# One level of Strassen's algorithm for both products of each MLP, in a two-layer trunk

## The chip, the cores and the metric

The kernel runs on one NeuronCore of one Trainium2 chip. The metric is the device time of one execution in microseconds, as the median of several runs. The core has five engines that work side by side, each through its own instructions in order: PE (matrix products and transposes), DVE (vector arithmetic), ACT (activation functions and copies), POOL (vector arithmetic and software-made DMAs) and SP (which issues DMAs). ACT and POOL issue DMAs too.

## The reference

A trunk of two layers over x (1024 tokens of 1024 numbers), with a token mixer (RWKV-7 beside Mamba-2 in layer 0, an mLSTM in layer 1), a cross-attention into 256 memory tokens, and an MLP of width 4096. The change concerns the MLP.

```python
def squared_relu_mlp(h, w_up, w_down):
    return jnp.square(jax.nn.relu(h @ w_up)) @ w_down

for i in range(DEPTH):
    ...
    x = x + rmsnorm(mix, norm_mix_post[i])
    ...
    x = x + rmsnorm(ca, norm_xa_post[i])
    ff = squared_relu_mlp(rmsnorm(x, norm_ff_pre[i]), ff_up[i], ff_down[i])
    x = x + rmsnorm(ff, norm_ff_post[i])
```

## The kernel before

**Products.** An fp32 product is made of three fp32r matmuls. `split` (L215) cuts a number into a high part, which ACT copies into fp32r (L217), and a low part, which DVE subtracts (L218). `mm3` (L207) multiplies high by high, high by low and low by high into one PSUM bank, through `mm` (L201); transposes go through `tr` (L205). Tiles of x are 128 tokens, so there are eight; a matmul here is 128x128 weights with 512 columns.

**Order.** A tile framework places the waits, and its scheduler, which simulates the program, fixes the order of each engine's instructions. The program hands it an order of its own as well: generators put on a list by `bg` are advanced by `tick` and `until`, by a model time `pt` that each matmul moves on. This is how norms of one stage run beside products of another.

**Cross-attention's end** (`xattn`). For each token tile the output product goes into a PSUM tile of 1024 columns (`psd`), `postnorm` (L337 to L363) squares it on ACT (L351), multiplies by the gain on DVE (L352), makes the reciprocal root on POOL (L354, L356), adds the residual on DVE (L362) and stores (L363). `tail_norm` then normalises for the MLP (`prenorm`, L334), and eight transposes with copies give the transposed x as high and low parts, `xth` and `xtl`.

**MLP** (`mlp`). The hidden width is cut into 16 chunks of 256. `up(c)` makes two times 128 hidden rows for all 1024 tokens, 48 matmuls each (`fm`), with Relu on ACT (L1439), a square on DVE (L1440) and a split into `u`. `down` multiplies a chunk's `u` by two rows of weights into a PSUM bank for each of 8 tiles and 2 column halves, and `add` copies (L1461) or adds (L1463) it on DVE into `acc`, which stays in SBUF. up(c+1) stands ahead of down(c). Weights of both products come by DMAs that ACT issues (`wstream`, L231), 512 KB each, and are split into `wb`. The first two up products begin with tokens 0 to 511 (`fm_two`) and take the rest when the last tiles of the attention are ready. The last two chunks are paired so that the tiles finish one after another; `finish(t)` is the post-norm and, in layer 0, the norm and transposes for layer 1. Each product has 1536 matmuls a layer, so both products of both layers have 6144.

## Time and profile before

| what | value |
|---|---|
| median of 3 runs | 3235.38 us (3228.02 to 3237.13) |
| the profiled execution's own time | 3245.01 us |
| its span, first to last instruction | 3243.2 us |
| mean granted TensorE clock | 0.982 |
| busy: PE, DVE, ACT, POOL | 3121.8, 1610.6, 1025.1, 342.6 us |
| DMA traffic | 361.54 MB, mean 111 GB/s |

The rows come from one execution recorded by the profiler. The span starts at the first instruction; the MLP of layer 0 runs from about 1147 to 1860 us of it, that of layer 1 from about 2520 us to the end. A row of the timeline gives start, length, engine, line, operation, output and inputs, shape and count, and in brackets how long the engine was idle just before and what ended the wait. The rows of a view by stretches give, after the stretch, the busy time of PE, PE's weight loads, DVE, ACT and POOL with their counts, the granted clock (1.00 is 2.4 GHz), the share of the 16 DMA engines in use and GB/s.

### The profile page before, as it was taken

What the parts mean: (1) busy time and instruction counts of PE and PEld (TensorE: products, weight loads), DVE (VectorE), ACT (ScalarE), POOL (GpSimd) and SP (SyncE); (2) the same over time, 40 slices, a digit from 0 to 9 for tenths busy, and PEclk for the clock granted to TensorE, in tenths of its full rate; (3) what the DMA queues carried; (4) which work ended last, traced back from release to release, by engine and by line L of the source; (5) the groups of instructions that cost most, each with busy time, mean ns of one, the idle gap of its engine ahead of it and who ended that gap; (6) DMA issues with size and microseconds to landing.
All of it is one profiled execution on the core that took longest, in us unless ns stands there. A gap on an engine that the chain in (4) does not pass through costs nothing. (4 is left out here: it accounts for less than half of the span.)

```text
span 3243.2 us, 40057 instructions
## 1 busy us (share of the span) xinstructions
PE 3121.8 (96%) x16420; PEld 2535.6 (78%) x16420; DVE 1610.6 (50%) x2247; ACT 1025.1 (32%) x1684; POOL 342.6 (11%) x444
## 2 busy tenths in 40 slices
PE   8999997889989999999999999899999999999999
PEld 8777676777768878888888788777788788888887
DVE  7255788566543444444444713146634444444445
ACT  6556533445333321111111413133433211111112
POOL 1111121122221100000000200012211000000001
PEclk9999998899989999999999999999999999999999
DMA  7734465588451221111111323455322211111112
GB/s 257 256 94 124 126 181 172 192 265 276 153 179 53 85 94 43 52 52 46 51 40 47 123 85 119 123 167 186 125 85 78 78 52 52 46 46 39 52 52 110
DMA packets 236295, 361.54 MB, mean 111 GB/s; under 512 B 54208, under 2 KB 157056, under 8 KB 236112
## 3 DMA queue, kind: packets, MB, share of 16 engines
q1 hardware_dynamic: 178832, 165.43, 16.8%
q10 hardware_dynamic: 45984, 152.59, 14.1%
q0 software_dynamic: 11296, 40.97, 3.2%
q8 instruction: 129, 2.11, 0.3%
q14 instruction: 54, 0.44, 0.0%
HBM read 262.73 MB, written 96.17 MB: 111 GB/s over the span
## 5 line engine op out<-in xcount | busy, mean ns | idle before, releaser
L201 PE MATMUL pd<-xth,wb 128*128 128x512 f32 x3168 | 1023.9, 398 | 15.9 <-DVE wb L218 13.6
L201 PE MATMUL pm<-wb,u 128*128 128x512 f32 x3072 | 738.1, 391 | 0.4 <-DVE acc L1463 0.4
L201 PEld LDWEIGHTS pd<-xth,wb 128*128 128x128 f32 x3168 | 596.6, 189 | 165.6 <-DVE wb L218 17.0
L201 PEld LDWEIGHTS pm<-wb,u 128*128 128x128 f32 x3072 | 576.5, 188 | 128.0 <-DVE acc L1463 1.3
L201 PE MATMUL pd<-xtl,wb 128*128 128x512 f32 x1600 | 635.4, 398 | 0.8 <-DVE xtl L218 0.8
L1463 DVE TENSOR_TENSOR acc<-pm,acc 128x512 f32<-128x512 f32 x448 | 305.5, 689 | 403.7 <-PE pm L201 403.7
L217 ACT ACTIVATE wb<-wr 128x1024 fp32r<-128x1024 f32 x244 | 252.8, 1051 | 701.8 <-PE pm L201 412.2
L218 DVE TENSOR_TENSOR wb<-wr,wb 128x1024 fp32r<-128x1024 f32 x244 | 295.4, 1224 | 227.9 <-ACT wb L217 227.4
L201 PEld LDWEIGHTS pd<-xtl,wb 128*128 128x128 f32 x1600 | 300.6, 188 | 73.3 <-issue 2.4
L201 PE MATMUL pd<-w,sh 128*128 128x512 f32 x1024 | 325.7, 400 | 8.6 <-DVE y L352 5.7
L201 PEld LDWEIGHTS pd<-w,sh 128*128 128x128 f32 x1024 | 193.6, 191 | 51.6 <-ACT w L217 5.9
L1440 DVE TENSOR_TENSOR ur<-ur 128x1024 f32<-128x1024 f32 x64 | 78.3, 1224 | 312.9 <-ACT ur L1439 312.9
L201 PE MATMUL pd<-w,sl 128*128 128x512 f32 x512 | 204.2, 399 | 0.0
L1439 ACT ACTIVATE ur<-pd 128x1024 f32<-128x1024 f32 x64 | 65.6, 1025 | 400.4 <-PE pd L201 400.4
L354 POOL TENSOR_SCALAR r<-ssh 128x1 f32<-128x1 f32 x48 | 25.4, 530 | 1553.8 <-ACT j L351 1553.0
L201 PE MATMUL pm<-wb,xth 128*128 128x512 f32 x512 | 163.1, 399 | 1.7 <-ACT wb L217 1.7
L201 PEld LDWEIGHTS pm<-wb,xth 128*128 128x128 f32 x512 | 96.6, 191 | 23.4 <-ACT wb L217 2.1
L201 PEld LDWEIGHTS pd<-w,sl 128*128 128x128 f32 x512 | 97.6, 191 | 21.8
L201 PE MATMUL pm<-wb,xtl 128*128 128x512 f32 x256 | 101.9, 398 | 0.0
L201 PE MATMUL ph<-w,mh 128*128 128x512 f32 x256 | 87.7, 419 | 3.9 <-ACT mh L217 3.0
L201 PE MATMUL pd<-w,yth 128*128 128x512 f32 x256 | 85.4, 412 | 2.9 <-DVE y L352 1.6
L218 DVE TENSOR_TENSOR u<-ur,u 128x1024 fp32r<-128x1024 f32 x64 | 78.2, 1221 | 1.1 <-ACT u L217 1.1
(344 smaller groups left out, 3628.8 us busy)
## 6 DMA issues: line engine op xcount, KB each, us to landing
wr<-in_ff_upT_dram ACTq DMA_DIRECT2D x64, 512.0 KB
wr<-in_ff_down_dram ACTq DMA_DIRECT2D x64, 512.0 KB
scr<-xo POOLq DMA_DIRECT2D x39, 512.0 KB, 3.0
scr<-mo POOLq DMA_DIRECT2D x32, 512.0 KB, 5.6
xo<-scr SPq DMA_DIRECT2D x32, 512.0 KB
wr<-in_ev_fm_dram ACTq DMA_DIRECT2D x26, 512.0 KB
wr<-in_xa_wkT_dram ACTq DMA_DIRECT2D x16, 512.0 KB
wr<-in_xa_wvT_dram ACTq DMA_DIRECT2D x16, 512.0 KB
```

Of the source, the lines that this page charges most:

```text
L201: self.nc.tensor.matmul(out, lhsT=lhsT, rhs=rhs, start=start, stop=stop)
L217: self.nc.scalar.activation(hi, src, AF.Copy)
L218: self.nc.vector.tensor_tensor(lo, src, hi.bitcast(F32), ALU.subtract)
L354: nc.gpsimd.tensor_scalar(r1[:], ss[:, 0:1], ss[:, 1:2], NORM_EPS, ALU.add, ALU.add)
L1439: nc.scalar.activation(r[:], ps[:], AF.Relu)
L1440: nc.vector.tensor_tensor(r[:], r[:], r[:], ALU.mult)
L1463: nc.vector.tensor_tensor(acc[:, t, sl], ps[:], acc[:, t, sl], ALU.add)
```

## The change

Both products of each MLP are made by one level of Strassen's algorithm in the form with seven products. Every matrix is cut into two by two blocks; seven block products replace eight, with sums and differences of blocks before and after. A product then has 1344 matmuls a layer.

*First product.* `half_norm` (L1443) replaces `tail_norm`: all tiles go to `xraw` as fp32, and tiles 0 to 3 are split as well, into `b1` (blocks B11, B21). `x_sums` (L1475) makes the other five right operands B22 and T1 to T4 tile by tile: four DVE subtractions (L1483) and five splits for each of four pairs of tiles. `prep` (L1498) loads the two weight rows of a pair of hidden chunks (512 KB each, issued on SP) and makes the left operands with four DVE sums and three and a half splits. `pair` (L1539) makes the seven block products, 12 matmuls each, for 256 hidden rows, adds them in PSUM and in `ub` (L1550 to L1574) and applies Relu and Square, and four POOL operations (L1576 to L1579) make the left operands of the second product. One DMA stores the seven pieces, 1792 KB, to the DRAM buffer `U` (L1580). `ub` has two buffers, used by pairs in turn. The products A11 x B11 and A12 x B21 of pairs 0 and 1 stand ahead, where fm_two stood.

*Second product.* It begins when all 16 pairs are done. There are 56 steps a layer, seven products by eight, each with 24 matmuls. `load` (L1619) brings one piece of U (`ru`) and one of weights (`rw`), 512 KB each (L1626, on SP), one step ahead in program order, and splits them into `wb` (four buffers) for two steps in five and into `sx` (three buffers) for the other three. `mul` makes six matmuls for each of four token tiles in a step. Products that share a result are summed in PSUM banks; at a product's end four banks are copied by ACT or added by DVE into `CA` and `CB` (L1686 to L1699). Tiles 0 to 3 finish during the last two products, tiles 4 to 7 at the end.

*Weight sums.* `down_sums` (L1423) makes the four sums and differences of blocks of ff_down, for both layers, as a background generator from the kernel's start: 64 times 512 KB in on SP, four POOL subtractions of 128x256, 512 KB out on POOL's queue, into the DRAM buffers `WS`. ff_down is laid out in blocks in DRAM (`ff_dn`). The scratch space for software-made DMAs is set to 4096.

The diff, cut to its core:

```diff
+        raw = qx.tile([P, NK, T], F32, name=self.n("xraw"), tag="xth")
+        b1 = qx.tile([P, 2, NK, 512], F32R, name=self.n("xb1"), tag="xtl")
+        xt = raw, (b1[:, 0], b1[:, 1])
...
-            self.bg(self.tail_norm(xo, g_ff, xt[0][:, :, ts], xt[1][:, :, ts], fin, 9.0))
+            self.bg(self.half_norm(t, xo, g_ff, xt, fin, 9.0))
...
+    def down_sums(self, l):
+        nc = self.nc
+        sub = ALU.subtract
+        for p in range(16):
+            for h in range(2):
+                w = self.cp.tile([P, 4, 256], F32, name=self.n("ws"), tag="ws")
+                cs = slice(256 * h, 256 * h + 256)
+                nc.sync.dma_start(w[:], self.A["ff_dn"][l, :, p // 2, :, p % 2, cs].rearrange("b p c -> p b c"))
+                yield 10.0
+                a1, a2, b1, b2 = [w[:, i, :] for i in range(4)]
+                op = lambda out, x, y: nc.gpsimd.tensor_tensor(out, x, y, sub)
+                op(a1, a2, a1)
+                op(a2, b2, a2)
+                op(b2, b2, a1)
+                op(b1, b1, b2)
+                nc.gpsimd.dma_start(self.WS[l][:, p // 2, :, p % 2, cs].rearrange("b p c -> p b c"), w[:])
+                yield 15.0
+        self.ws_done[l] = True
...
+            if t < 4:
+                self.split(hi[:, ks, ts], lo[:, ks, ts], v)
+            self.nc.scalar.copy(raw[:, ks, ts], v)
...
+        wb = self.pool(ca, "wb", 4, side)
...
+        def x_sums():
+            for t in range(4):
+                yield lambda: 0.0 if cond(t + 5) else None
+                yield 1.5
+                c = slice(P * t, P * t + P)
+                r11, r21 = [raw[:, 4 * i:4 * i + 4, c] for i in range(2)]
+                r12, r22 = [raw[:, 4 * i:4 * i + 4, 512 + P * t:640 + P * t] for i in range(2)]
+                sp = lambda k, src: self.split(X[k][0][:, :, c], X[k][1][:, :, c], src)
+                op = lambda out, x, y: nc.vector.tensor_tensor(out, x, y, sub)
+                sp("B22", r22)
+                op(r11, r12, r11)
+                op(r12, r22, r12)
+                op(r22, r22, r11)
+                sp("T2", r22)
+                sp("T1", r11)
+                op(r21, r21, r22)
+                sp("T3", r12)
+                sp("T4", r21)
...
+        def prep(p):
+            d = {}
+            fa = self.wr.tile([P, 1024], F32, name=self.n("wr"), tag="wr")
+            nc.sync.dma_start(fa[:], A["ff_upT"][l, 2 * p])
+            fb = self.ed.tile([P, 1024], F32, name=self.n("wf"), tag="gain")
+            nc.sync.dma_start(fb[:], A["ff_upT"][l, 2 * p + 1])
+            def first():
+                t1 = sp2()
+                self.split(t1[:, 0], t1[:, 1], fa[:])
+                d["A11"], d["A12"] = cut(t1)
+            def rest():
+                s = self.ed.tile([P, 1024], F32, name=self.n("ws"), tag="xn")
+                nc.vector.tensor_tensor(s[:, lo], fb[:, lo], fb[:, hi], add)
+                nc.vector.tensor_tensor(s[:, hi], s[:, lo], fa[:, lo], sub)
+                t2 = sp2()
+                self.split(t2[:, 0], t2[:, 1], s[:])
+                d["S1"], d["S2"] = cut(t2)
+                if "A11" not in d:
+                    first()
+                s4 = self.ed.tile([P, 1024], F32, name=self.n("ws"), tag="xo")
+                nc.vector.tensor_tensor(s4[:, lo], fa[:, lo], fb[:, lo], sub)
+                nc.vector.tensor_tensor(s4[:, hi], fa[:, hi], s[:, hi], sub)
+                t3 = sp2()
+                self.split(t3[:, 0], t3[:, 1], s4[:])
+                d["S3"], d["S4"] = cut(t3)
+                t4 = sp2()
+                self.split(t4[:, 0, lo], t4[:, 1, lo], fb[:, hi])
+                d["A22"] = t4[:, 0, lo], t4[:, 1, lo]
+            return d, first, rest
...
+        def prod(ps, w, x, start=True):
+            for k in range(4):
+                c = slice(P * k, P * k + P)
+                self.mm3(ps, (w[0][:, c], w[1][:, c]), (x[0][:, k, :], x[1][:, k, :]), start and k == 0, k == 3, not start)
...
+        def pair(p, d, early=None, ahead=None):
+            u = ub[:, p % 2]
+            sl = lambda i: u[:, i, :]
+            if early is None:
+                ab = self.psd()
+                a, b = ab[:, lo], ab[:, hi]
+            else:
+                (a, a2), b = early, self.psm()[:]
+            c = self.psm()[:]
+            prod(b, d["S2"], X["T2"])
+            nc.scalar.copy(sl(7), b)
+            prod(c, d["S1"], X["T1"])
+            if ahead is not None:
+                ahead()
+            if early is None:
+                prod(a, d["A11"], X["B11"])
+            nc.scalar.copy(sl(3), a)
+            nc.vector.tensor_tensor(sl(7), sl(7), sl(3), add)
+            prod(b, d["S3"], X["T3"], False)
+            nc.vector.tensor_tensor(sl(2), b, sl(3), add)
+            nc.vector.tensor_tensor(sl(2), c, sl(2), add)
+            if early is None:
+                prod(a, d["A12"], X["B21"], False)
+                nc.scalar.activation(sl(0), a, AF.Relu)
+            else:
+                nc.vector.tensor_tensor(sl(0), a2, sl(3), add)
+                nc.scalar.activation(sl(0), sl(0), AF.Relu)
+            prod(b, d["A22"], X["T4"], False)
+            nc.vector.tensor_tensor(sl(1), b, sl(3), add)
+            nc.scalar.activation(u[:, 1:3], u[:, 1:3], AF.Relu)
+            nc.scalar.activation(u[:, 0:3], u[:, 0:3], AF.Square)
+            prod(c, d["S4"], X["B22"], False)
+            nc.vector.tensor_tensor(sl(7), c, sl(7), add)
+            nc.scalar.activation(sl(7), sl(7), AF.Relu)
+            nc.scalar.activation(sl(7), sl(7), AF.Square)
+            op = nc.gpsimd.tensor_tensor
+            op(sl(3), sl(7), sl(2), add)
+            op(sl(4), sl(3), sl(0), sub)
+            op(sl(5), sl(0), sl(7), sub)
+            op(sl(6), sl(1), sl(4), sub)
+            nc.sync.dma_start(U[:, p // 2, :, p % 2, :].rearrange("i p c -> p i c"), u[:, 0:7])
...
+        for d, first, rest in pre:
+            first()
+        for d, first, rest in pre:
+            ab = self.psd()
+            early.append((ab[:, lo], ab[:, hi]))
+            prod(early[-1][0], d["A11"], X["B11"])
+            prod(early[-1][1], d["A12"], X["B21"])
+        pre[0][2]()
+        self.until(lambda: xdone[0])
+        ub = qx.tile([P, 2, 8, 512], F32, name=self.n("ub"), tag="xth")
...
+            if p >= 1 and p + 1 < NP:
+                nxt[0] = prep(p + 1)
+                pre.append(nxt[0])
+            pair(p, pre[p][0], early[p] if p < 2 else None, ahead if p + 1 < NP else None)
+        ctx.close()
+        self.until(lambda: self.ws_done.get(l))
...
+        pr = self.pool(cs, "fr", 3, side)
+        px = self.pool(cs, "fx", 3, side)
...
+        prods = [(0, dn[0]), (4, WS[3]), (1, dn[2]), (3, WS[0]), (6, dn[3]), (5, WS[1]), (2, WS[2])]
+        steps = [(i, q) for i in range(7) for q in range(NP // 2)]
+        got = []
+        def load(n):
+            while len(got) <= min(n, len(steps) - 1):
+                i, q = steps[len(got)]
+                slot, w = prods[i]
+                pairs = []
+                for src, tag in ((U[slot, q], "ru"), (w[q], "rw")):
+                    r = pr.tile([P, 1024], F32, name=self.n(tag), tag=tag)
+                    nc.sync.dma_start(r[:], src.rearrange("p q c -> p (q c)"))
+                    t = sp2() if len(got) % 5 < 2 else px.tile([P, 2, 1024], F32R, name=self.n("sx"), tag="sx")
+                    self.split(t[:, 0], t[:, 1], r[:])
+                    pairs.append(cut(t))
+                got.append(pairs)
...
+        for i in range(7):
+            if i in (0, 3):
+                bank_a = [self.psm()[:] for _ in range(4)]
+            if i == 1:
+                bank_b = [x for d_ in (self.psd(), self.psd()) for x in (d_[:, lo], d_[:, hi])]
...
+            bank = bank_a if i in (0, 2, 3, 4) else bank_b
+            start = i in (0, 1, 3)
+            for q in range(NP // 2):
+                n = i * (NP // 2) + q
+                if i == 6 and q == NP // 2 - 2:
+                    load(n + 1)
+                    for t in range(4):
+                        for z in range(2):
+                            mul(q + z, t, bank[t], got[n + z], False)
+                    break
+                load(n + 1)
+                for t in range(4):
+                    mul(q, t, bank[t], got[n], start)
+                got[n] = None
...
+    nc = _bacc.Bacc("TRN2", target_bir_lowering=False, num_devices=1, dynamic_dma_scratch_size=4096)
```

**DVE at the MLP's start.** The rows are DVE's in layer 0, from the end of the last tile's post-norm (y is its product by the gain, xo its sum, xn its normalised form). Before:

```order
L352 TENSOR_TENSOR y_9884<-pd_9797,gain_9197 128x512 [waits Activation_49] x2
L362 SCALAR_TENSOR_TENSOR xo_9882<-y_9884,r_1709_9894,xo_9882 128x1024 [waits DMASW6_49,DMAHW3_49,DVE_49,Pool_49]
...
L352 TENSOR_TENSOR y_9971<-pd_9898,gain_9197 128x512 [waits Activation_49]
L218 TENSOR_TENSOR wb_10002<-wr_10000,wb_10002 128x1024 [waits DMAHW5_49,Activation_49]
L218 TENSOR_TENSOR wb_10007<-wr_10005,wb_10007 128x1024 [waits DMAHW6_49,Activation_49]
L218 TENSOR_TENSOR xtl_9196<-pm_9952,xth_9195 128x4x128 [waits Activation_49]
```

Now (xraw, B and T are the blocks of x and their splits; ws and wb are weight sums and splits):

```order
L362 SCALAR_TENSOR_TENSOR xo_10113<-y_10115,r_1745_10125,xo_10113 128x1024 [waits DMASW7_49,DMAHW4_49,DVE_49,Pool_49]
L218 TENSOR_TENSOR T_1752_10142<-xraw_9311,T_1752_10142 128x4x128 [waits Activation_49]
L1483 TENSOR_TENSOR xraw_9311<-xraw_9311 128x4x128 [waits DVE_49]
L218 TENSOR_TENSOR T_1751_10141<-xraw_9311,T_1751_10141 128x4x128 [waits Activation_49]
L1521 TENSOR_TENSOR ws_10278<-wr_10144,wf_10146 128x512 [waits DMAHW5_49,DMASW0_49]
...
L334 SCALAR_TENSOR_TENSOR xn_10162<-xo_10113,r_1764_10167,gain_9315 128x1024 [waits PE_49,Pool_49]
...
L1483 TENSOR_TENSOR xraw_9311<-xraw_9311 128x4x128 [waits Activation_49]
...
L1483 TENSOR_TENSOR xraw_9311<-xraw_9311 128x4x128 [waits DVE_49,Activation_49]
L1514 TENSOR_TENSOR ws_10334<-ws_10334,wr_10148 128x512 [waits DVE_49]
L218 TENSOR_TENSOR T_1749_10139<-xraw_9311,T_1749_10139 128x4x128 [waits Activation_49]
```

Between the last tile's sum and its normalised form now stand eight operations of x_sums and prep, and its own x_sums stand behind further weight sums and splits.

**SP at the change from the first to the second product**, in layer 0. The first row is the store of pair 14, ru and rw are the loads of the second product; before, SP issued no weights in an MLP:

```order
L1580 DMA scr_10143<-ub_10306 128x7x512 [waits DVE_49,DMAHW7_49,Activation_49,Pool_49]
L1626 DMA ru_12335<-scr_10143 128x1024 [waits DMAHW0_49,PE_49]
L1626 DMA rw_12340<-in_ff_dn_dram 128x1024 [waits DMAHW1_49]
L1626 DMA ru_12345<-scr_10143 128x1024 [waits DMAHW2_49]
L1626 DMA rw_12350<-in_ff_dn_dram 128x1024 [waits DMAHW3_49,PE_49]
L1626 DMA ru_12379<-scr_10143 128x1024 [waits DMAHW4_49]
...
L1626 DMA ru_12452<-scr_10143 128x1024 [waits DMAHW2_49,DVE_49]
L1580 DMA scr_10143<-ub_10306 128x7x512 [waits Pool_49]
L1626 DMA rw_12457<-in_ff_dn_dram 128x1024 [waits DMAHW3_49,DVE_49]
```

The loads stand behind the store of pair 14, and the store of pair 15 stands behind the load of step 4's ru.

**PE and ACT at steps 2 to 5 of the second product.** Before, a down product's matmuls of layer 0 (wb is weights, u the hidden values, pm the bank):

```order
L201 MATMUL pm_10535<-wb_10219,u_10214 128x512 x2
L201 MATMUL pm_10535<-wb_10407,u_10274 128x512 x3
L201 MATMUL pm_10543<-wb_10219,u_10214 128x512 x3
L201 MATMUL pm_10543<-wb_10407,u_10274 128x512 x3
L201 MATMUL pm_10551<-wb_10219,u_10214 128x512 x3
L201 MATMUL pm_10551<-wb_10407,u_10274 128x512 x3
```

Now PE's rows:

```order
L201 MATMUL pm_12331<-sx_12386,sx_12381 128x512 [waits Activation_49]
L201 MATMUL pm_12331<-sx_12386,sx_12381 128x512 [waits DVE_49]
L201 MATMUL pm_12331<-sx_12386,sx_12381 128x512 x4
...
L201 MATMUL pm_12334<-sx_12386,sx_12381 128x512 x6
L201 MATMUL pm_12331<-sx_12425,sx_12420 128x512 [waits Activation_49]
L201 MATMUL pm_12332<-sx_12425,sx_12420 128x512
L201 MATMUL pm_12333<-sx_12425,sx_12420 128x512
L201 MATMUL pm_12334<-sx_12425,sx_12420 128x512
L201 MATMUL pm_12331<-sx_12425,sx_12420 128x512 [waits DVE_49]
L201 MATMUL pm_12331<-sx_12425,sx_12420 128x512 x4
...
L201 MATMUL pm_12331<-sx_12459,sx_12454 128x512 [waits Activation_49]
```

and ACT's splits:

```order
L217 ACTIVATE sx_12381<-ru_12379 128x1024 [waits DMAHW4_49]
L217 ACTIVATE sx_12386<-rw_12384 128x1024 [waits DMAHW5_49]
L217 ACTIVATE sx_12420<-ru_12418 128x1024 [waits DMAHW6_49]
L217 ACTIVATE wb_12488<-ru_12486 128x1024 [waits DMAHW3_49,DVE_49,PE_49]
L217 ACTIVATE wb_12493<-rw_12491 128x1024 [waits DMAHW4_49,DVE_49]
L217 ACTIVATE sx_12425<-rw_12423 128x1024 [waits DMAHW7_49,DVE_49,PE_49]
L217 ACTIVATE sx_12454<-ru_12452 128x1024 [waits DMAHW0_49,DVE_49]
L217 ACTIVATE wb_12524<-ru_12522 128x1024 [waits DMAHW5_49]
L217 ACTIVATE wb_12529<-rw_12527 128x1024 [waits DMAHW7_49]
L217 ACTIVATE sx_12459<-rw_12457 128x1024 [waits DMAHW2_49,DVE_49,PE_49]
```

Where down matmuls ran on without a wait, the first matmul of a step now waits for ACT and one a little later for DVE; ACT's splits into sx wait for PE where the buffer was read by the step before, and those of steps 5 and 6 into wb stand between.

## Rows read from the trace of the kernel before

**Rows 1.** The page's first lines: the span, busy time of each engine and its share.
```profile
span 3243.2 us, 40057 instructions
...
PE 3121.8 (96%) x16420; PEld 2535.6 (78%) x16420; DVE 1610.6 (50%) x2247; ACT 1025.1 (32%) x1684; POOL 342.6 (11%) x444
```
**Rows 2.** Busy time in two stretches: us; busy PE, PEld, DVE, ACT, POOL; clock, DMA share, GB/s.
```profile
1200.00:1790.00 590.00, 590.00 (x2552) 479.75 (x2552) 266.31 (x321) 107.06 (x106) 0.00 (x0) 1.00 0.14 47
2598.00:3190.00 592.00, 592.00 (x2563) 481.09 (x2562) 266.70 (x318) 109.96 (x109) 0.00 (x0) 1.00 0.14 48
```
**Rows 3.** The page's groups: busy us, mean ns of one, idle before, its releaser.
```profile
L201 PE MATMUL pm<-wb,u 128*128 128x512 f32 x3072 | 738.1, 391 | 0.4 <-DVE acc L1463 0.4
...
L1463 DVE TENSOR_TENSOR acc<-pm,acc 128x512 f32<-128x512 f32 x448 | 305.5, 689 | 403.7 <-PE pm L201 403.7
L217 ACT ACTIVATE wb<-wr 128x1024 fp32r<-128x1024 f32 x244 | 252.8, 1051 | 701.8 <-PE pm L201 412.2
L218 DVE TENSOR_TENSOR wb<-wr,wb 128x1024 fp32r<-128x1024 f32 x244 | 295.4, 1224 | 227.9 <-ACT wb L217 227.4
```
**Rows 4.** Busy time in three stretches of the mixers, columns as above.
```profile
0.00:50.00 50.00, 38.41 (x254) 34.56 (x255) 33.59 (x40) 31.66 (x49) 12.22 (x26) 1.00 0.85 286
150.00:1150.00 1000.00, 926.92 (x6273) 743.27 (x6273) 592.37 (x804) 432.43 (x762) 184.99 (x204) 0.95 0.50 159
650.00:800.00 150.00, 137.32 (x1749) 116.09 (x1746) 94.82 (x193) 75.48 (x168) 34.77 (x42) 0.94 0.85 277
```
**Rows 5.** Timeline of PE at the first MLP's start: start us, us, operation, idle before.
```profile
1147.08 1.03 PE L205 MATMUL pm<-ct,xn 128*128 128x128 f32 x8
1148.36 0.73 PE L201 MATMUL pd<-xth,wb 128*128 128x512 f32 x2 [0.25 <-ACT xth L217]
1149.44 0.50 PE L201 MATMUL pd<-xtl,wb 128*128 128x512 f32 x1 [0.35 <-DVE xtl L218]
```
**Rows 6.** Timeline of DVE there, and at the layer change.
```profile
1148.70 1.28 DVE L218 TENSOR_TENSOR xtl<-pm,xth 128x512 fp32r<-128x512 f32 x2
...
1819.26 1.28 DVE L362 SCALAR_TENSOR_TENSOR xo<-yn,r,xo 128x1024 f32<-128x1024 f32 x1
```
**Rows 7.** POOL by shapes: a 128x512 operation with two inputs.
```profile
L884 POOL TENSOR_TENSOR M<-M,ea 128x512 f32<-128x512 f32 x6 | 6.3, 1042 | 62.8 <-ACT ea L863 62.8
```
**Rows 8.** The page's DMA issues: queue, count, KB each, us to landing.
```profile
scr<-xo POOLq DMA_DIRECT2D x39, 512.0 KB, 3.0
```
**Rows 9.** Timeline of PE in layer 1's mixer, round a long idle.
```profile
2056.69 1.16 PE L201 MATMUL pm<-qk 64*128 64x128 f32 x8 [0.25 <-ACT vo L1288]
2066.07 0.48 PE L205 MATMUL pm<-ct,g 8*128 8x8 f32 x3 [8.22 <-DMA g<-scr]
```
**Rows 10.** Busy time round PE's idles at 1821 and 2058, columns as above.
```profile
1820.00:1826.00 6.00, 2.92 (x17) 2.25 (x17) 5.18 (x7) 2.96 (x8) 2.34 (x6) 1.00 0.28 107
2065.00:2070.00 5.00, 3.93 (x11) 3.20 (x12) 2.44 (x10) 1.06 (x1) 0.36 (x1) 0.50 0.88 232
2070.00:2075.00 5.00, 5.00 (x21) 3.80 (x19) 0.00 (x0) 0.00 (x0) 2.01 (x1) 0.77 0.51 158
```
**Rows 11.** Timeline of PE at the layer change.
```profile
1824.41 1.09 PE L205 MATMUL pm<-ct,xn 128*128 128x128 f32 x8 [3.08 <-DVE xn L334]
...
1863.82 0.50 PE L201 MATMUL pm<-wb,xth 128*128 128x512 f32 x1 [1.70 <-ACT wb L217]
```
**Rows 12.** Timeline of the last tile's end.
```profile
3236.15 0.69 DVE L1463 TENSOR_TENSOR acc<-pm,acc 128x512 f32<-128x512 f32 x1 [0.23 <-PE pm L201]
...
3239.52 1.00 SPq L360 DMA_DIRECT2D out_dram<-xth  x2
```
**Rows 13.** Timeline of POOL and DVE in layer 1's mixer.
```profile
2161.79 2.36 POOL L1186 TENSOR_TENSOR G<-G,ct 128x1024 f32<-128x1024 f32 x1 [5.51 <-ACT G L1184]
...
2223.43 3.75 POOL L1186 TENSOR_TENSOR G<-G,ct 128x1024 f32<-128x1024 f32 x1 [5.93 <-ACT G L1184]
...
2222.77 2.19 DVE L1250 SCALAR_TENSOR_TENSOR ly<-ly,r,so 128x128 f32<-128x128 f32 x8
```

More of the change, by code (lines that the diff above doesn't have):

```diff
@@ L1445, in up @@
-        def up(c):
-            if c == 0:
-                us = [act(ps) for ps in self.fm_two([ws(0), ws(1)], xt, cond)]
-            else:
-                us = [act(self.fm(ws(2 * KC * c + j), xt)) for j in range(KC)]
-            return us
-        def down(ps, t, h, us, wd, first, last):
-            ts, sl = slice(128 * t, 128 * t + 128), slice(512 * h, 512 * h + 512)
-            n = len(us)
-            for j in range(n):
-                self.mm3(ps[:], (us[j][:, 0, ts], us[j][:, 1, ts]), (wd[j][0][:, sl], wd[j][1][:, sl]), first and j == 0, last and j == n - 1)
@@ new lines, in mlp, with ahead @@
+        pre = [prep(p) for p in range(2)]
+        early = []
+        for d, first, rest in pre:
[8 more added lines that the diff above has]
+        ub = qx.tile([P, 2, 8, 512], F32, name=self.n("ub"), tag="xth")
+        nxt = [pre[1]]
+        def ahead():
+            nxt[0][2]()
@@ new lines, in mlp @@
+        for p in range(NP):
+            if p >= 1 and p + 1 < NP:
[4 more added lines that the diff above has]
+        self.until(lambda: self.ws_done.get(l))
+        pc = self.pool(ca, "fc", 1, side)
+        CA = [pc.tile([P, T], F32, name=self.n("ca"), tag=f"a{t}") for t in range(4)]
+        CB = [pc.tile([P, T], F32, name=self.n("cb"), tag=f"b{t}") for t in range(4)]
@@ L1465, in finish, with mul @@
+        def mul(q, t, ps, uw, start):
+            for j in range(2):
+                (u, w) = uw[0][j], uw[1][j]
+                c = slice(P * t, P * t + P)
+                self.mm3(ps, (u[0][:, c], u[1][:, c]), w, start and q + j == 0, q == NP // 2 - 1 and j == 1, not start)
+        fin = [0]
+        xt_next = g_next = None
+        xres = [None] * NT
         def finish(t):
@@ L1539, in run, with sums @@
         prev = ExitStack()
+        def sums():
+            for l in range(2):
+                yield from self.down_sums(l)
+        self.bg(sums())
         mem = KP[1], VP[1], base, w0
```

150 lines of the change are left out of this document (76 added, 74 removed).

## The prediction

> **What bounds the kernel now.** I read the busy shares first: PE is busy in 3121.8 of 3243.2 us [rows 1]. Then the stretches of the two MLPs: in 590 us and 592 us of them PE is never idle and its granted clock is 1.00 [rows 2], 590 / 2552 = 0.231 us a matmul. The groups say why nothing else matters there: DVE stands idle 403.7 us for PE ahead of its additions, ACT 701.8 us ahead of the weight splits, most of it for PE, while all 3072 down matmuls lost 0.4 us [rows 3]. So in an MLP the matmul count is the time, and every wait the change puts before a matmul is added to it. The mixers are another matter: there DMA fills 0.85 of its engines in the stretches of [rows 4].
>
> **The change, part by part**, against the profiled execution's own 3245.0 us (span 3243.2).
>
> *Matmuls removed.* Each product falls from 1536 to 1344, four products: 768 fewer, as the order of instructions has it. 768 x 0.231 = **-177.5**.
>
> *Start of each MLP.* Before, the first matmul on the last tile starts after two idles of 0.25 and 0.35 us [rows 5]: one copy, one subtraction. Now that tile passes x_sums first. By the order, DVE has 16 operations (14 of 512 elements at 0.60, a pitch taken a little under half of the 1.28 us for two in [rows 6], and two of 1024 at the 1.28 of its last row) between the last product of the attention and the last xn: 11 us, and about 1 more for the reciprocal root on POOL that stands between them. PE has 46 matmuls (10.6 us) to do meanwhile: 2 us idle, with the wait for DVE at the first of them. Then transposes and copies of 1.6 us and eight operations to T1's low part (seven at 0.60, one at 1.22), 5.4 us: 7 us idle; 0.6 us more at T2. 9.6 us each, **+19** (10 to 30).
>
> *From first to second product.* SP issues in program order: the loads of step 0 stand behind the store of pair 14. That pair's chain: eviction 0.69, Relu on 1024 and Square on 1536 elements 2.6 (ACT's 1.05 per 1024 of [rows 3]), four POOL sums at 1.04 [rows 7] to 1.3, the store of 1792 KB at the 286 GB/s of [rows 4] 6.4 and about 1.4 of latency (512 KB land in 3.0 us [rows 8], 1.8 at that rate with a little over 1 left), the load of 1 MB 3.2, the split 1.1: 20 to 21 us with little overlap. PE has 58 matmuls, 13.6 us, beside it: 8 us idle each, **+16** (8 to 30).
>
> *Clock.* After PE's idle of 8.22 us [rows 9] the granted clock was 0.50 and 0.77 in the next two stretches of 5 us, about 3 us lost; round an idle of 3.08 us it stayed 1.00 [rows 10]. Four long idles, some in two parts: **+8** (0 to 15).
>
> *Second product.* Nothing of it was streamed from DRAM before; 56 steps a layer, each 24 matmuls (5.5 us) on one 128x1024 piece of U and one of weights. Loads (1 MB in 5.5 us, 190 GB/s) and splits (ACT 2.1, DVE 2.4 us [rows 3]) fit by volume. Not by order: three steps in five put their splits in three sx buffers, so in 20 steps of a layer the second split has to wait until the matmuls of the step just ahead end. Then PE waits for ACT 1.05, and for DVE 1.22 less the high-part matmuls it can do meanwhile (four in 11 steps: 0.92; two in 9: 0.46), with three hand-overs of about 0.1, an estimate under the 0.25 and 0.35 us of [rows 5], which hold some of the copy itself: 1.67 and 2.13 us. 11 x 1.67 + 9 x 2.13 = 37.5, two layers **+75** (0 if the split runs ahead after all; 90 if no matmul does). Clock: nothing, by the 3.08 us above.
>
> *First product.* A pair is 84 matmuls, 19.7 us, with ACT about 9 and DVE about 10 us beside them (counted by the 1.05 and 1.22 of [rows 3], halved for 512 elements); the extra arithmetic costs nothing while PE covers it. One loop is tight: ub has two buffers, so pair p+2's copy into it (L1556) waits until pair p's store has landed. From the product on T4: 0.69 + 2.6 + 4.2 to 5.2 + 7.8, with hand-overs 16 to 17 us, against 72 matmuls, 16.9 us. The copy may come a little late; PE waits only if it is some 2.6 us late, since 24 matmuls (5.6 us) stand ahead of the next use of the bank, and from them go the copy (0.6), two DVE operations behind it (1.4) and about 1 us in ACT's and DVE's queues. **+5** (0 to 90, rival B). Weights issued on SP in place of ACT: nothing, ACT idles.
>
> *down_sums.* 64 times 512 KB in, four POOL subtractions, 512 KB out, all before layer 0's MLP, in stretches where DMA stands at 0.85 [rows 4]. 64 MB at 286 GB/s is 234 us of transfer; the mean share of 0.50 from 150 to 1150 us leaves room for it. Most hides beside PE; what waits on DMA there, or on POOL's queue (256 subtractions of about 0.5 us, half of [rows 7]), does not: **+20** (0 to 60).
>
> *Rest.* Bank turnovers between products +4. The layer change loses its idles of 3.08 and 1.70 us [rows 11] in part, as next-layer matmuls fall in before the last step: -4. The last tile's chain after the last matmul, from its last addition at 3236.15 to the end [rows 12], is the same: 0.
>
> Sum: -177.5 + 19 + 16 + 8 + 75 + 5 + 20 + 4 - 4 = -34.5, so 3210.5 for an execution like the profiled one. That one stands 9.6 us above the median of 3235.38; on the median the forecast is 3235.4 - 34.5 = 3200.9, rounded **3200**. A difference under 0.3% (9.7 us) can't be told from none.
>
> **Rivals.**
> *A, the waits are covered.* In before's MLP, splits of the same size cost PE nothing [rows 2, 3]. If the hardware's order of arrival lets most sx splits run early, the 75 become 25, and if the sums hide wholly, 20 become 10: 3140. Against it: ACT and DVE run in order, and a buffer that PE is reading can't be filled.
> *B, the ub loop takes the first product (the other side).* For it: POOL's 128x1024 operation took 2.36 us alone, and 3.75 us where it began during a DVE operation [rows 13], 1.39 longer. If each of the four sums waits for a DVE operation that way, the chain grows by 5.2 us; if the store, with 1 MB of weights loading beside it, moves at two thirds of 286 GB/s, by 3.2 more. 8.4 less the 2.6 of room is 5.8 per turn, and a turn is two pairs: 2.9 x 32 = 93 in place of 5, 3288. It decides from 2.6 us on; POOL's growth alone gives 1.3 x 32 = 42, 3237. Against it: DVE is idle half of each pair, so not every sum meets an operation.
> The Trainium skill states a rule that speaks for B (SBUF — State Buffer, "SBUF: two separate sides"): a DVE operation with two SBUF inputs and a GpSimd operation that reads SBUF share a port pair as an exclusive lock, and the later one "fully blocks". The 3.75 us row agrees: the POOL operation seems to have stood still for what was left of the DVE one. By that rule at its worst the sum gives B's 3288, by the 1.04 us of an undisturbed operation the forecast's 3200.
> *C, the sums slow the mixers.* 64 MB more where DMA already stands at 0.85, and POOL's small operations of the norms queue behind four subtractions each time: 60 where I put 20, 3240. Against it: the scheduler spreads them, and PE is idle only 4% now [rows 1].
> *D, the saving isn't there*: 768 fewer matmuls stand in the order, so only a lower clock or stretched matmuls could do it; near 3235.
>
> **How the numbers follow.** Forecast (3165 to 3225) 0.54, A 0.16, B 0.15, C 0.12, D 0.03. The likeliest is the forecast, 3200. The range 3135 to 3280 takes in A to its lower part, C, and half of B; about 0.16 lies outside. Faster by over 0.3% (under 3225.7): A, and 0.52 of the forecast's 0.54, 0.68. Slower by over 0.3% (over 3245): B's 0.15 less its mild end, half of C and the far end of the mixers' price, 0.22. Between: 0.10.
>
> **What would show it.** Right: about 1.7 to 2.1 us of PE idle at 20 second-product steps a layer, with ACT's sx split as releaser, summing to 60 to 90 us; PE without a gap in the pairs of the first product, at 19.7 us each; 7 to 10 us idle at each MLP's start and at each change to the second product; PE matmuls 768 fewer. A: those idles absent. B: PE waiting in each pair, POOL sums well over 1.3 us, pairs over 21 us. C: the MLP of layer 0 starting over 40 us later than the 1147 us of [rows 5]. Wrong as a whole: a loss in the MLPs that is none of these waits, such as matmuls that take longer than 0.231 us at a granted clock of 1.00, or loads of U that land late for many steps.

## The result, and the profile after

The changed kernel takes 3400.77 us (median of 4 runs, 3396.53 to 3403.64) beside 3236.26 us for the kernel before: a ratio of 1.0511, 95% interval 1.0486 to 1.0535. It is 5% slower where 1% faster was forecast, and 121 us above the range's upper end.

The page's first lines, which answer to [rows 1]:

```profile
span 3394.8 us, 40400 instructions
...
PE 3028.6 (89%) x15652; PEld 2424.4 (71%) x15652; DVE 1690.5 (50%) x2243; ACT 1329.1 (39%) x2085; POOL 831.4 (24%) x900
```

PE has 768 matmuls fewer and 93 us less of busy time, and yet the span is 151.6 us longer. The next step is to see in which stage. The starts of the stages are first and last matmuls in PE's timeline. Before, the first row of layer 0's MLP, its last, and the first of layer 1's (start, length, operation):

```profile
1134.94 0.50 PE L201 MATMUL pd<-xth,wb 128*128 128x512 f32 x1 [0.93 <-ACT wb L217]
```

```profile
1854.84 2.21 PE L201 MATMUL pm<-wb,u 128*128 128x512 f32 x9
```

```profile
2523.19 0.50 PE L201 MATMUL pd<-xth,wb 128*128 128x512 f32 x1 [0.93 <-ACT wb L217]
```

After: the first product of layer 0's MLP, the last row of that product, the first and the last row of its second, the first product of layer 1's MLP:

```profile
1280.07 0.74 PE L201 MATMUL pd<-xb,wb 128*128 128x512 f32 x2 [0.93 <-ACT wb L217]
```

```profile
1620.03 2.88 PE L201 MATMUL pd<-T,wb 128*128 128x512 f32 x12
```

```profile
1628.29 2.07 PE L201 MATMUL pm<-wb,wb 128*128 128x512 f32 x4 [5.38 <-ACT wb L217]
```

```profile
1997.17 1.52 PE L201 MATMUL pd<-wb,wb 128*128 128x512 f32 x6
```

```profile
2669.24 0.73 PE L201 MATMUL pd<-xb,wb 128*128 128x512 f32 x2 [0.93 <-ACT wb L217]
```

Put together, in us (the columns of three experiments that follow are read from the same places):

| stage | before | after | e1: no sums | e8: no sums, buffers in turn | e12: paced sums |
|---|---|---|---|---|---|
| to the first MLP's first matmul | 1134.9 | 1280.1 | 1148.3 | 1148.2 | 1147.2 |
| MLP of layer 0 | 722.1 | 718.6 | 716.8 | 666.0 | 681.2 |
| of that, first / second product | | 342.8 / 375.8 | 343.6 / 373.2 | 344.2 / 321.8 | 358.6 / 322.6 |
| layer 1's mixer and attention | 666.1 | 670.5 | 668.7 | 669.3 | 684.0 |
| MLP of layer 1, to the end | 720.0 | 725.5 | 724.5 | 671.9 | 675.4 |
| span | 3243.2 | 3394.8 | 3258.3 | 3155.4 | 3187.8 |

Two things are to be explained. Nearly the whole loss, 145.1 us, lies before the first MLP, where the change adds little but the weight sums. And the MLPs, which have 177.5 us of matmuls less, are no shorter: -3.5 and +5.5 us.

**Before the MLP.** Busy time up to its first matmul (columns as in [rows 2]), before and after:

```profile
0.00:1134.90 1134.90, 1045.87 (x7076) 852.47 (x7076) 657.75 (x874) 509.64 (x858) 211.18 (x254) 0.96 0.54 172
```

```profile
0.00:1280.10 1280.10, 1076.64 (x7077) 868.73 (x7077) 690.95 (x875) 514.14 (x867) 490.87 (x574) 0.91 0.66 205
```

As many matmul records. PE's busy time is 31 us longer at a lower granted clock (0.91 for 0.96), and the idle time, span less busy, has gone from 89 to 203 us. POOL has 280 us more work. The groups of the page show what it is, and that one subtraction costs 954 ns:

```profile
L1434 POOL TENSOR_TENSOR ws<-ws 128x256 f32<-128x256 f32 x256 | 244.3, 954 | 425.8 <-DMA ws<-in_ff_dn_dram 403.7
```

The list of waits, POOL's and SP's (engine, line, waits for what: us in total, times, longest):

```profile
POOL ws L1434 <- DMA ws<-in_ff_dn_dram: 403.7, 54, 13.4
```

```profile
SPq L1431 <- DMA scr<-ws: 417.5, 51, 20.2
```

So POOL stood 403.7 us in 54 waits at the sums' subtractions until a load had landed (there are 64 rounds), and SP 417.5 us at the next load until the store before had landed. What that does to the mixer is seen in one place. POOL's timeline, the last operation on DVE that L545 depends on (it reads the xn that L545 overwrites), and PE's row there:

```profile
492.49 0.94 POOL L599 MEMSET Ts<- 128x1024 f32 x1
493.49 0.16 POOL L600 MEMSET Ts<- 128x32 f32 x1
499.60 3.48 POOL L1434 TENSOR_TENSOR ws<-ws 128x256 f32<-128x256 f32 x2 [5.95 <-DMA ws<-in_ff_dn_dram]
503.04 2.33 POOL L545 TENSOR_TENSOR xn<-xn,km 128x1024 f32<-128x1024 f32 x1
```

```profile
493.49 1.21 DVE L544 TENSOR_TENSOR bk<-xn,gain 128x1024 f32<-128x1024 f32 x1
```

```profile
505.43 1.22 PE L201 MATMUL pm<-xn,rkw 128*128 128x512 f32 x1 [8.92 <-POOL xn L545]
```

POOL is done with the memsets at 493.65 and stands 5.95 us for the sums' load. The mixer's own operation L545 is behind two subtractions in its queue: DVE was done at 494.70, POOL begins L545 at 503.04, 8.3 us later (in e1 it begins 0.1 us behind DVE's end), and PE waits 8.92 us for it. Other long idles of PE bear names such as DVE xn, ACT mo or ACT sh in the list of waits. I haven't followed each of them through the queues; the experiments measure their sum.

**The second product.** PE's timeline round four of the steps whose split waits for the step before (the first two have four matmuls to do before they need the low part, the others two), with three steps between that wait for nothing:

```profile
1649.60 6.09 PE L201 MATMUL pm<-sx,sx 128*128 128x512 f32 x24 [1.15 <-ACT sx L217]
1656.84 6.10 PE L201 MATMUL pm<-sx,sx 128*128 128x512 f32 x24 [1.15 <-ACT sx L217]
1662.77 11.04 PE L201 MATMUL pm<-wb,wb 128*128 128x512 f32 x48
1673.65 5.60 PE L201 MATMUL pm<-sx,sx 128*128 128x512 f32 x24
1680.40 0.73 PE L201 MATMUL pd<-sx,sx 128*128 128x512 f32 x2 [1.15 <-ACT sx L217]
1681.66 6.86 PE L201 MATMUL pd<-sx,sx 128*128 128x512 f32 x22 [0.53 <-DVE sx L218]
1689.66 0.73 PE L201 MATMUL pd<-sx,sx 128*128 128x512 f32 x2 [1.15 <-ACT sx L217]
1690.92 5.28 PE L201 MATMUL pd<-sx,sx 128*128 128x512 f32 x22 [0.53 <-DVE sx L218]
1696.04 4.24 PE L201 MATMUL pd<-wb,wb 128*128 128x512 f32 x18
```

The waits are those that were forecast. Their idle looks a little short: 1.15 us with four matmuls (1.67 forecast), 1.15 + 0.53 with two (2.13). But the idle isn't all that a wait costs. Steps without one follow each other at 5.44 us (10.88 for the two from 1662.77); from 1649.60 to 1656.84 it is 7.24, so 1.80 us are lost, at a granted clock of 1.00 (the row from 1648). The rows' lengths hold the part that the idle doesn't: 6.09 us for 24 matmuls in place of 5.60.

A second thing adds to it: behind the wait for the low part the 22 matmuls take 6.86 us in one step and 5.28 in the next. The stretches of 2 us tell why (columns as in [rows 2]):

```profile
1648.00:1656.00 8.00, 6.48 (x26) 4.38 (x25) 5.77 (x6) 4.39 (x6) 0.00 (x0) 1.00 0.81 259
1682.00:1684.00 2.00, 2.00 (x7) 1.63 (x6) 1.04 (x1) 0.00 (x0) 0.00 (x0) 0.60 0.70 219
1684.00:1686.00 2.00, 2.00 (x6) 1.55 (x6) 0.00 (x0) 0.00 (x0) 0.00 (x0) 0.54 0.78 227
1690.00:1692.00 2.00, 1.47 (x7) 0.91 (x6) 2.00 (x2) 0.56 (x1) 0.00 (x0) 1.00 0.05 6
```

The granted clock was 0.60 and 0.54 after the first pair of idles, near the lower of its two levels (1.2 GHz), and 1.00 after the second. From 1673.65 to 1696.04 three steps take 22.4 us for 16.3 at 5.44; the low clock is 1.6 of the 6.1 lost (6.86 less 5.28), and 4.5 are left for the two steps, 2.2 each for 2.13 forecast.

**The rest of the MLP.** Its start, for which 9.6 us of idle were forecast:

```profile
1281.33 5.41 PE L201 MATMUL pd<-xb,wb 128*128 128x512 f32 x22 [0.52 <-DVE wb L218]
1289.09 7.42 PE L201 MATMUL pd<-xb,wb 128*128 128x512 f32 x24 [2.34 <-DVE y L352]
1300.72 1.97 PE L205 MATMUL pm<-ct,xn 128*128 128x128 f32 x8 [4.22 <-DVE xn L334]
1305.36 0.80 PE L201 MATMUL pm<-T,wb 128*128 128x512 f32 x1 [2.67 <-ACT T L217]
1309.20 16.03 PE L201 MATMUL pm<-T,wb 128*128 128x512 f32 x60 [3.04 <-DVE T L218]
```

The last three are the waits named (the last xn, T1's high part, its low part): 4.22 + 2.67 + 3.04 = 9.9, with 2.34 ahead of them. The 60 matmuls of the last row then take 0.267 us each. The change to the second product idles 5.38 us (the row at 1628.29) where 8 were forecast. In the pairs PE hardly waits. The granted clock is 0.86 in the 50 us that hold the end of it, and 1.00 with PE never idle later:

```profile
1300.00:1350.00 50.00, 41.34 (x168) 33.24 (x168) 38.59 (x51) 24.84 (x33) 11.76 (x8) 0.86 0.33 114
1450.00:1500.00 50.00, 50.00 (x218) 40.36 (x217) 28.07 (x36) 23.97 (x28) 16.51 (x12) 1.00 0.35 121
```

### The profile page after: what moved, and what is told of

Same layout as the page of the kernel before. It is cut to its first block, busy times and chain, and to the rows that moved or that the text cites. A ratio compares the mean times of both kernels' runs of the same rounds, so it can differ in the third digit from the quotient of the medians.

```text
span 3394.8 us, 40400 instructions
## 1 busy us (share of the span) xinstructions
PE 3028.6 (89%) x15652; PEld 2424.4 (71%) x15652; DVE 1690.5 (50%) x2243; ACT 1329.1 (39%) x2085; POOL 831.4 (24%) x900
## 5 line engine op out<-in xcount | busy, mean ns | idle before, releaser
L201 PE MATMUL pd<-xth,wb 128*128 128x512 f32 x1120 | 369.6, 406 | 36.1 <-DVE wb L218 14.8
L218 DVE TENSOR_TENSOR wb<-wr,wb 128x1024 fp32r<-128x1024 f32 (+1 forms) x148 | 190.1, 1290 | 339.9 <-ACT wb L217 339.5
L1434 POOL TENSOR_TENSOR ws<-ws 128x256 f32<-128x256 f32 x256 | 244.3, 954 | 425.8 <-DMA ws<-in_ff_dn_dram 403.7
L201 PEld LDWEIGHTS pd<-xth,wb 128*128 128x128 f32 x1120 | 215.7, 194 | 95.2 <-DVE wb L218 16.3
L201 PE MATMUL pd<-T,wb 128*128 128x512 f32 x1008 | 247.7, 397 | 16.7 <-DVE wb L218 12.8
L201 PE MATMUL pm<-sx,sx 128*128 128x512 f32 x912 | 222.2, 395 | 24.2 <-ACT sx L217 22.9
L201 PEld LDWEIGHTS pd<-T,wb 128*128 128x128 f32 x1008 | 189.1, 190 | 66.8 <-DVE wb L218 19.6
L201 PE MATMUL pd<-xtl,wb 128*128 128x512 f32 (+1 forms) x576 | 234.7, 409 | 0.0
L201 PE MATMUL pd<-sx,sx 128*128 128x512 f32 x672 | 183.5, 427 | 37.7 <-ACT sx L217 20.0
L201 PE MATMUL pd<-xb,wb 128*128 128x512 f32 x768 | 193.7, 402 | 9.3 <-DVE y L352 4.7
L1576 POOL TENSOR_TENSOR ub<-ub 128x512 f32<-128x512 f32 x32 | 43.1, 1346 | 487.1 <-ACT ub L1570 412.4
```

Source lines behind the costliest of these rows:

```text
L201: self.nc.tensor.matmul(out, lhsT=lhsT, rhs=rhs, start=start, stop=stop, skip_group_check=on)
L218: self.nc.vector.tensor_tensor(lo, src, hi.bitcast(F32), ALU.subtract)
L1434: op = lambda out, x, y: nc.gpsimd.tensor_tensor(out, x, y, sub)
L1576: op(sl(3), sl(7), sl(2), add)
```

## The experiments

All runs stand beside runs of the kernel before on the same chip; the medians of before were 3233.9 to 3234.5 us.

**e1, without the weight sums.** The second product loads unsummed blocks in their place.

```diff
-        self.bg(sums())
-        self.until(lambda: self.ws_done.get(l))
-        prods = [(0, dn[0]), (4, WS[3]), (1, dn[2]), (3, WS[0]), (6, dn[3]), (5, WS[1]), (2, WS[2])]
+        prods = [(0, dn[0]), (4, dn[3]), (1, dn[2]), (3, dn[0]), (6, dn[3]), (5, dn[1]), (2, dn[2])]
```

> The weight sums are left out altogether, and the second product loads unsummed blocks of ff_down in their place (same sizes), so the output is not the reference's. The trace of the changed kernel has the first MLP starting 145 us late (1280.07 for 1134.94 us), the rest of the span within 7 us of before. Theory: all of those 145 us are the background sums'. Then 3401 - 145 = about 3255, and the first matmul of the MLP at about 1135 to 1140 us. Rival: the mixer is slow for another reason of the change (its weights, its DMA scratch space, the scheduler's different order), then 3350 or more.

3258.63 us, ratio 1.0076 (1.0051 to 1.0100). The sums cost 142 us. The MLP still starts 13.4 us later than before; no run separates what that is (the other order that the scheduler finds, the other DMA scratch space, the new norms).

**e2 and e3, copies alone and subtractions alone.** e2 leaves out the four lines `op(...)` of L1435 to L1438. e3 loads one buffer once, subtracts 256 times on it and neither loads nor stores again; its second product loads unsummed blocks.

> Loads and stores of the weight sums stay, the four subtractions between are left out (the sums' buffers hold plain blocks). Theory queues: SP and POOL stand behind the load and the store of the one ws buffer, so little is won, 3340 to 3390. Rival traffic (128 MB... 64 MB moved beside the mixers) says the same, 3350 to 3400. Rival arithmetic: POOL's 244 us of subtractions and what they do to DVE are the price, then 3260 to 3290.

> The opposite: 256 subtractions on POOL stay at the same places of the program, on one buffer loaded once; the 63 other loads and all 64 stores of the sums are left out, and the second product loads unsummed blocks. Theory queues and rival traffic: 3260 to 3290, since POOL never waits for a load nor SP for a store. Rival arithmetic: 3360 to 3400.

3359.42 us (1.0390, 1.0363 to 1.0417) and 3324.44 us (1.0281, 1.0257 to 1.0304). Neither alone is the price: over e1 the copies cost 101 us and the subtractions 66, together 142. These are not the parts' prices at the changed kernel's places, for the scheduler crowds them: the last load of the sums is issued at 862 us in e2 and at 1158 in the changed kernel. e2 lies in the ranges of both the queues and the traffic and doesn't tell them apart; e3 lies between the ranges of both its theories. Without loads to wait for, 233 of the 256 subtractions begin in the first 300 us, and POOL is full there:

```profile
0.00:300.00 300.00, 250.28 (x1381) 206.66 (x1382) 156.20 (x127) 145.74 (x177) 266.74 (x298) 0.94 0.52 171
```

The mixer's operations on POOL stand in that queue as well. So the price isn't the wait for a DMA alone.

**e5, an eighth of the bytes.** Loads, subtractions and stores on 16 partitions (`w[:16]`) in the same number; the second product loads unsummed blocks.

> All loads, subtractions and stores of the weight sums stay, on 16 of the 128 partitions: the same instructions and waits, an eighth of the bytes; the second product loads unsummed blocks. With all sums out the kernel took 3258.6, with the subtractions alone 3324.4, with the copies alone 3359.4, with both 3400.8. Theory queues: what costs is that SP and POOL stand still until a load or store has landed; small DMAs land sooner, so most of the copies' part goes and the subtractions' part stays: 3315 to 3340. Rival order: it is the mere place of these instructions in the mixer's queues (the scheduler's other order), not the length of the waits: 3370 to 3400.

3331.05 us (1.0294, 1.0267 to 1.0320): seven eighths of the traffic taken away bring 70 of 142 us, about to the price of the subtractions alone. It doesn't tell shorter waits from less traffic, since both shrink.

**e7, the loads on POOL's queue** (`nc.gpsimd.dma_start` for `nc.sync.dma_start` at L1431).

> As the changed kernel, but the sums' loads are issued on POOL's queue instead of SP's. In the trace of the changed kernel SP stands 417.5 us at these loads, waiting for the store before, and the mixers' own loads behind it. Theory SP: that is most of the price, 3320 to 3350. Rival POOL: POOL's 403.7 us of standing for the loads is the price, and each load now costs POOL 0.8 us more: 3390 to 3430.

3401.62 us (1.0516, 1.0492 to 1.0540), unchanged. SP is free of the sums, but now POOL stands for loads and for stores:

```profile
POOL ws L1434 <- DMA ws<-in_ff_dn_dram: 252.8, 57, 10.9
POOL ws L1431 <- DMA scr<-ws: 216.7, 53, 13.6
```

**e4 and e8, the buffers in turn**, e8 with the sums left out as well.

```diff
-                    t = sp2() if len(got) % 5 < 2 else px.tile(...
+                    t = sp2() if len(got) % 2 < 1 else px.tile(...
```

> In the second product the steps take wb and sx buffers in turn, so that no split has to wait for the step just ahead. Theory: the 40 exposed splits cost what their waits sum to in the trace of the changed kernel, 57 us of waits for ACT's and DVE's sx splits plus some for wb, so 3401 - 55 to 75 = about 3330 to 3345. Rival: the loads land too late for that as well, and the waits move to DMA: 3380 to 3400.

> The sums left out as in e1 and the buffers in turn as in e4; the output is not the reference's. If the two costs are separate they add: 3258.6 - 103 = about 3155, 80 us below before: what the matmuls saved are worth once both are gone, less the MLP's starts. Rival: they overlap, since e4 won more than the waits on sx sum to (103 for about 60) and part of it came from elsewhere: 3180 to 3200.

3297.38 us (1.0197, 1.0173 to 1.0222), 103 us less than the changed kernel, and 3154.13 us (0.9753, 0.9730 to 0.9776). The costs add, to within a microsecond of the 3155 expected. e4's second product, to be held against the changed kernel's:

```profile
1628.30:1998.70 370.40, 336.31 (x1400) 264.61 (x1400) 168.67 (x156) 136.55 (x165) 26.66 (x30) 0.97 0.52 172
```

```profile
1634.00:1949.60 315.60, 314.91 (x1393) 260.35 (x1394) 167.53 (x155) 135.90 (x163) 28.02 (x29) 0.99 0.60 201
```

Idle goes from 34.1 to 0.7 us and PE's busy time from 336.3 to 314.9 us for as many matmuls (1344 of the second product in each; the other records are of layer 1's beginning). Of these 21 us the granted clock explains about 8: 0.03 of 370 us was withheld before, 0.01 of 316 now. The other 13 are the part of the waits that stands in the rows' lengths.

**e6, layer 1's sums later.** With e4's buffers; one tiny copy on POOL makes layer 1's first load depend on the last tile of layer 0's MLP input.

> The alternating buffers of e4 and, besides, layer 1's sums held back until the last tile of layer 0's x has passed into the MLP (one tiny copy makes the first load depend on it). All sums are made. Theory: the mixer of layer 0 pays only for the sums that remain in it (21 of 64 rounds by the order), about a third of 142 us, and the MLP pays little for the others, since POOL has 134 us of work in 710 there: 3297 - 90 = about 3205. Rival: in the MLP the sums' loads and stores stand in SP's and POOL's queues ahead of the stores and loads of U, and the first product waits in each pair: 3250 to 3300.

3318.40 us (1.0257, 1.0227 to 1.0288), 21 us worse than e4. The mixer's part fell to 31 us over e1, but the first and second product grew to 388.4 and 386.3 us: the sums' rounds now stand among U's stores and loads. In the first product PE waits for the copy into ub (L1556, here L1558), which is rival B's loop; in the changed kernel that was 1.9 us in two waits:

```profile
PE pd L201 <- ACT ub L1558: 22.3, 11, 5.0
```

The expectation of 3205 fell; the rival held in kind, though the time lies above its 3250 to 3300.

**e9 to e12, the same sums at a pace.** With e4's buffers; nothing left out. The load and the first subtraction of each round are pinned in their engine's order behind what the program had issued before them, so that the numbers at `yield` decide where they stand:

```diff
-                nc.sync.dma_start(w[:], self.A["ff_dn"]...
-                yield 10.0
+                keep(nc.sync.dma_start(w[:], self.A["ff_dn"]...
+                yield 5.0
...
-                op(a1, a2, a1)
+                keep(op(a1, a2, a1))
...
-                yield 15.0
+                yield 5.0
```

with `keep = self.tc.keep_in_program_order`; e10 has 9 and 6, e11 9 and 6 for layer 0 and 20 and 16 for layer 1, e12 12 and 8 and 20 and 16.

> The alternating buffers of e4, and the sums' load and first subtraction of each round pinned in SP's and POOL's order behind what the program issued before them, at a pace of 5 and 5 units of model time (10 to 15 us in the mixers) instead of wherever the scheduler's simulation found the engine idle; all sums are made, same bytes, same arithmetic. By the order, 13 rounds move into layer 0's first product. Theory queues: the price is POOL standing for a load that the schedule took as landed; with the pacing most of that goes, and 3297 falls to 3220 to 3255. Rival arithmetic and traffic: the 256 subtractions and 64 MB cost what they cost anywhere: 3280 to 3300.

> As e9 at a slower pace, 9 and 6 units, so that loads have more time to land before POOL comes to them; 30 rounds move behind the first layer's mixer and attention. Theory queues: POOL's standing falls further in the mixer and little is paid in the MLP: 3210 to 3245. Rival: in the MLP the pace is 15 us a round, too short for the round trip of about 17 us, and SP stands at the sums' loads ahead of U's stores and loads, as with e6: 3260 to 3300.

> As e10 for layer 0's sums (9 and 6 units); layer 1's at 20 and 16, so that a round has twice its round trip of some 17 us and the rest spread through layer 0's MLP, layer 1's mixer and attention. In e10 the MLP of layer 0 took 54 us more than with the sums out, the mixer of layer 0 15 more. Theory queues: with twice the round trip SP and POOL hardly stand, most of the 54 us comes back, and layer 1's mixer pays about as little a round as layer 0's did (15 us for some 30): 3180 to 3200. Rival: the sums cost wherever they are by DMA and arithmetic, and layer 1's mixer pays what the MLP saves: 3215 to 3230.

> As e11 with layer 0's sums at 12 and 8 units. Theory queues: a little less in the mixer, but some of layer 0's rounds move into its first product, where a round costs more: within 15 us of e11 either way. If pace alone counted it would be 10 us below e11.

| run | us | ratio (95% interval) | sums' loads issued ahead of the first MLP | its start, over e1's |
|---|---|---|---|---|
| e4, unpaced | 3297.38 | 1.0197 (1.0173 to 1.0222) | 64 | +137.7 |
| e9 | 3257.10 | 1.0076 (1.0060 to 1.0093) | 48 | +50.3 |
| e10 | 3224.62 | 0.9965 (0.9952 to 0.9979) | 33 | +14.8 |
| e11 | 3194.35 | 0.9877 (0.9859 to 0.9894) | 33 | +14.5 |
| e12 | 3190.70 | 0.9864 (0.9843 to 0.9885) | 26 | -1.1 |

e9's 3257 missed its range by 2 us. From e4 to e9 three quarters of the rounds remain in the stage and a third of their price: 2.2 us a round becomes 1.0, and 0.4 in e10. All arithmetic and all bytes are still there in e12, and 37 us (e12 less e8) are left of 143 (e4 less e8); the other 106 went with the place and the pace of the sums. Two rivals can be held against the stretches up to the first MLP, e1's, e9's and e10's (columns as in [rows 2]):

```profile
0.00:1148.30 1148.30, 1039.93 (x7077) 843.79 (x7077) 659.84 (x875) 512.08 (x866) 210.48 (x254) 0.95 0.54 170
```

```profile
0.00:1198.60 1198.60, 1053.44 (x7077) 857.73 (x7077) 673.85 (x875) 514.14 (x868) 431.10 (x489) 0.94 0.66 204
```

```profile
0.00:1163.10 1163.10, 1041.93 (x7076) 847.89 (x7076) 689.35 (x875) 512.68 (x867) 367.16 (x419) 0.94 0.64 197
```

If a fuller DMA were the price, e9 would pay it: its DMA share and rate (0.66, 204 GB/s) are the changed kernel's (0.66, 205), at 50 us over e1 in place of 132 (the changed kernel) and 138 (e4). If it were DVE slowing beside POOL, e10 would: DVE is busy 689 us in it, 691 in the changed kernel, 660 in e1, and e10 pays 15. What no run separates is how the price divides between loads that POOL waits for, subtractions ahead of the mixer's operations, and transfers that meet at one moment; e9 to e12 change the pinning, the pace and the number of rounds together. An estimate from the changed kernel's trace: followed back through what released it, 54 of PE's 202 us of idle up to the first MLP pass through a load, subtraction or store of the sums; e1 has 107 us of idle there in all.

POOL's waits for the sums' loads in e12, up to the first MLP, from there to its end, and from there to the second:

```profile
POOL ws L1435 <- DMA ws<-in_ff_dn_dram: 69.5, 8, 22.4
```

```profile
POOL ws L1435 <- DMA ws<-in_ff_dn_dram: 130.0, 6, 32.8
```

```profile
POOL ws L1435 <- DMA ws<-in_ff_dn_dram: 125.7, 6, 55.1
```

It still stands for the loads, but in layer 0's mixer for 69.5 us in place of 403.7. What is left of the price lies in the other two stretches: by the table of stages layer 0's first product is 14.4 us longer than e8's, and layer 1's mixer and attention 14.7. **e12 beats both kernels: 1.4% faster than before, 6% faster than the changed one.**

## Why the prediction was wrong

- *Matmuls removed, -177.5*: right. There are 768 records fewer, and steps without a wait follow at 5.44 us, 0.227 a matmul. e8, without the sums and the exposed splits, is 80 us below before, with the starts and the changes paid.
- *down_sums, +20 (0 to 60)*: **the step that failed**. It measured 142 us, over twice its upper end. I costed bytes against a DMA share and 256 subtractions at 0.5 us beside PE. A subtraction took 954 ns, but the work and the bytes as such were the smaller part (37 us are left of 143 in e12): POOL and SP run in order, and the sums' waits and subtractions stood ahead of the mixer's operations, as at L545. The prediction even named POOL's queue, but gave it no row of its own. The order printed only where the sums stand, not that POOL would stand there for its load 7.5 us a time (403.7 us in 54). C had the place and half the mechanism, the queue behind the subtractions without the waits for their loads, at 60 us and with 0.12; that "the scheduler spreads them" spoke for the forecast was the wrong way round.
- *Second product, +75 (0 to 90)*: the mechanism was right, the size too small. e4 removes 33 and 32 us of idle in the two layers, but 108 us of time went with it (375.8 to 321.0 and 368.2 to 315.1). In the steps followed above a wait costs 1.8 and 2.2 us by the starts, for 1.67 and 2.13. The second term that failed is "Clock: nothing, by the 3.08 us above": one idle that left the clock at 1.00 did not price forty waits. By the granted clock it is 8 to 9 us a layer, some 18 of the 108. The 90 that are left, for 75, are waits of these steps and of others; they were not counted one by one.
- *Start of each MLP, +19, and clock, +8*: the idle was right (9.9 us for 9.6, 2.34 us more ahead), the sum too small. The two first products took 342.8 and 343.4 us where 1344 matmuls at 0.231 are 310.5: 65 us over both. Before's MLPs lay 16 us over theirs (722.1 and 712.9 for 3072 x 0.231), so at least 49 are new, for 32 forecast with the +5 of the ub loop. PE's idle in them is 22 and 23 us; the granted clock, 0.97 over each, withheld 10 us in each, some of it while PE was idle. So the clock's +8 was mis-sized as well.
- *From first to second product, +16*: about 12, the 6.1 and 6.3 us of idle that e4's second products keep.
- *The end, 0*: wrong by 7. From PE's last matmul to the end it is 13.9 us, 7.1 before: the four last tiles end close together and stand in DVE's and POOL's queues.
- *Before and between the MLPs*: with the sums out the first MLP still starts 13.4 us late (e1), for which the prediction has no row. With it the terms come to about 190 of the 199 us between forecast and result.
- *Rival B* did not come. The growth that it was built on was read from one row of POOL, 3.75 us [rows 13]; the DVE row beside it is not one operation but eight (x8). POOL's four sums did lengthen beside DVE, from 1.04 [rows 7] to 1.35 to 1.61 us:

```profile
L1578 POOL TENSOR_TENSOR ub<-ub 128x512 f32<-128x512 f32 x32 | 51.5, 1611 | 0.0
...
L1577 POOL TENSOR_TENSOR ub<-ub 128x512 f32<-128x512 f32 x32 | 44.6, 1394 | 0.0
...
L1579 POOL TENSOR_TENSOR ub<-ub 128x512 f32<-128x512 f32 x32 | 44.5, 1389 | 2.5
...
L1576 POOL TENSOR_TENSOR ub<-ub 128x512 f32<-128x512 f32 x32 | 43.1, 1346 | 487.1 <-ACT ub L1570 412.4 <-DVE wb L218 74.7
```

Four together grew by about 1.6 us, below the 2.6 from which it would decide, and PE waited 1.9 us for the copy into ub in layer 0's first product. The trace agrees with the direction of the Trainium skill's rule (SBUF — State Buffer, "SBUF: two separate sides"), not with its worst case.

## What to carry to other kernels

Work put in the background of an in-order engine is not priced by its own time, but by what stands behind it while it waits for a DMA: look for the waits of every queue that it enters, and at which of its neighbours PE needs next. Where a scheduler's order leaves an engine standing for loads, pin such work to the program's order and spread its rounds, as e9 to e12 did; moving it to an idler stage without that moved the loss here (e6). And a buffer rotation in which a split's target was read by the step just ahead costs the split and more: count which step last used each buffer before counting buffers, and price a wait by the starts of the steps, not by the idle column alone.
